# Row tiles of the seven-product stages: split three ahead into x's leftover tiles, loaded into four raw tiles

## The chip, the cores and the metric

One core of a Trainium2 chip. The metric is the device time of one execution in microseconds: 2548.99 us is the median of three runs before the change (2543.51 to 2549.86).

## The reference

One decoder layer of sliding-window attention, on x of 2048 tokens by 2048 channels, all float32:

```
h = rms_norm(x, swa_norm)
q, k, v, gate = split(h @ w_in, [2048, 2304, 2560])   # w_in 2048 x 4608, 32 query heads of 64, 4 key heads
q, k = rms_norm(q, q_gain), rms_norm(k, k_gain)       # per head
for each block of 128 queries, its keys being its own block and the one before:
    s = q @ k^T / 8 + bias[bucket(dist)], outside the window of 128: -inf
    m = max(max(s), sink); p = exp(s - m); p = p / (sum(p) + exp(sink - m))
    o = p @ v
x + (o * silu(gate)) @ w_out                          # w_out 2048 x 2048
```

The change touches two matrix products of it alone, each 2048 x 2048 x 2048: the gate's part of h @ w_in, and the last one with w_out.

## The kernel before

**Numbers in two parts.** Every float32 operand is split into a high part h (a copy rounded to TensorE's float32r format) and a low part l (the remainder, also float32r), and a product is the sum of three: h with h, h with l, l with h. For a row tile (128 output rows, held as the stationary operand) the parts are called wh and wl, made by `split_stat` (L123): for each half of 512 columns a copy on ScalarE (L133), then a subtraction on VectorE (L134). The moving operand's parts are called bigh and bigl, later obh and obl (`add_operand`, L536). `gemm` (L141) runs, for each k tile of 128, six matmuls of 128 x 512 columns: wh with the operand's high part (L148), wh with its low part (L151), wl with its high part (L154), each for two column halves.

**Two parts of the program.** In the first (up to about 1207 us) queries, keys and values are projected and attention runs beside the projections; its output goes to DRAM as `o_sp`. The second computes two large products one after the other: stage "g" (the gate projection, multiplied into `o_sp`, giving `o2_sp`) and stage "o" (times w_out, plus x). Each is done by a scheme with seven products of half size (1024 x 1024 x 1024) in place of eight, in the order b11, b21, t2, t3, t4, t1, b22 (L641). A product is named by its moving operand. Each has eight row tiles of 128 rows, and a row tile takes 8 k tiles x 6 = 48 matmuls into two accumulators of PSUM. In b11 and b21 of stage "g" the operand is what is left of x in SBUF from the projections; the other twelve operands are built by `prepare` (L564) while the product before them runs, one k tile beside each row tile.

**Row tiles.** `stationary` (L590) loads a row tile's raw values of 128 x 1024 (512 KB). For b11, b21 and t4 that is one load. For t3, t1 and b22 two loads are added or subtracted on VectorE (in the trace araw<-araw,a2raw, L498). For t2 three are loaded, one subtraction runs on GpSimd (L501), one addition on VectorE, and the sum is also stored to DRAM (`s2_sp`, L599), from where b22 fetches it again. The first raw tile comes from four buffers called raw, the second (a2raw) from four called rest: the buffers that hold the last two k tiles of x's second half until product b21 of stage "g" is done. Row tiles are loaded up to two products ahead (L667), in t2 of "g" only one ahead after the first. They are split when their own product is issued (L588), and wh and wl have three buffers of half a row tile each.

**Results.** Each product's accumulators are added to or stored as running sums (u in SBUF, u3 through DRAM). The products b21, t4, t1 and b22 also finish output tiles: in "g" by gating (VectorE, ScalarE, GpSimd, then a store of craw), in "o" by adding x (a load of x into craw, GpSimd, VectorE, then a store of craw; L639). PSUM has eight accumulators there, two for each row tile.

**The order.** Tiles come from pools with a fixed number of buffers. The program text gives the priority, a planner simulates the engines and puts every engine's instructions into one fixed order, and semaphores are added after that. All transfers are issued by SyncE (SP), in order: one that waits for a buffer holds those behind it. VectorE, ScalarE and GpSimd work in order as well.

The lines that the change touches besides `load_a2` (L510) and `product` (L586):

```
        if name == "t2":
            other = load_a if kind == "g" and i == 0 else load_a2
            a11, a21, a22 = [f(quarter_a(kind, mh, kh, i)) for f, mh, kh in ((other, 0, 0), (other, 1, 0), (load_a, 1, 1))]
...
        while made < min(len(tiles), m + 3) and not (made > m + 1 and tiles[made][0] == 2 and tiles[made][1] > 0):
            raws.append(stationary(*flat[tiles[made][0]], tiles[made][1]))
            made += 1
```

Of the kernel before, what the change touches and what calls it, by code (L numbers as in the profile page):

```python
# [16 lines left out]
P = 128  # L17
# [5 lines left out]
CH = 512  # L23
# [8 lines left out]
def swa_layer_kernel(ctx: ExitStack, tc: tile.TileContext, xT: bass.AP, x: bass.AP, w_in: bass.AP,  # L32
# [90 lines left out]
    def split_stat(raw, cuts=(0, HALF), eng=nc.vector):  # L123

        parts = []
        for n in range(2):
            h = st.tile([P, CH], F32R, tag="wh", name="wh", bufs=3)
            l = st.tile([P, CH], F32R, tag="wl", name="wl", bufs=3)
            for a, b in zip(cuts, cuts[1:]):
                a, b = max(a - n * CH, 0), min(b - n * CH, CH)  # L130
                if a < b:
                    r = raw[:, n * CH + a:n * CH + b]
                    nc.scalar.copy(out=h[:, a:b], in_=r)  # L133
                    eng.tensor_tensor(out=l[:, a:b], in0=r, in1=h[:, a:b].bitcast(F32), op=ALU.subtract)  # L134
            parts.append((h, l))
        return parts
# [4 lines left out]
    def gemm(stat, res, acc=None, ks=range(KT), last=KT - 1):  # L141
        if acc is None:
            acc = new_acc()
        for k in ks:
            h, l = stat[k // 4]
            cs = slice((k % 4) * P, (k % 4 + 1) * P)
            for n in range(2):
                nc.tensor.matmul(acc[n], h[:, cs], res[0][k][:, n * CH:(n + 1) * CH],  # L148
                                 start=(k == 0), stop=False)
            for n in range(2):  # L150
                nc.tensor.matmul(acc[n], h[:, cs], res[1][k][:, n * CH:(n + 1) * CH],  # L151
                                 start=False, stop=False)
            for n in range(2):
                nc.tensor.matmul(acc[n], l[:, cs], res[0][k][:, n * CH:(n + 1) * CH],  # L154
                                 start=False, stop=(k == last))
        return acc
# [346 lines left out]
    def bring(raw, src):  # L503
        nc.sync.dma_start(out=raw if len(src.shape) == 2 else raw.rearrange("p (k c) -> p k c", c=P), in_=src)  # L504
        return raw
# [1 line left out]
    def load_a(src):  # L507
        return bring(st.tile([P, HALF], F32, tag="raw", name="araw", bufs=RAW), src)

    def load_a2(src):  # L510
        return bring(rest.tile([P, HALF], F32, tag="rest", name="a2raw"), src)

    def load_b(src):
        return bring(gp.tile([P, HALF], F32, tag="braw", name="braw", bufs=3), src)

# [67 lines left out]
            vec(raw, raw, b, ALU.subtract)  # L583
        add_operand(ops, raw, scale if kind == "g" else None)

    def product(raw, ops, accs):  # L586
        acc = [accs.tile([P, CH], F32, tag="acc", name="acc") for _ in range(2)]
        return gemm(split_stat(raw), ops, acc, ks=range(8), last=7)  # L588

    def stationary(kind, name, i):  # L590

        if name in ("b11", "b21", "t4"):
            return load_a(quarter_a(kind, *{"b11": (0, 0), "b21": (0, 1), "t4": (1, 1)}[name], i))
        if name == "t2":
            other = load_a if kind == "g" and i == 0 else load_a2
            a11, a21, a22 = [f(quarter_a(kind, mh, kh, i)) for f, mh, kh in ((other, 0, 0), (other, 1, 0), (load_a, 1, 1))]
            pool(a11, a21, a11, ALU.subtract)
            vec(a22, a22, a11, ALU.add)
            nc.sync.dma_start(out=s2_sp[i], in_=a22)  # L599
            return a22  # L600
        a = load_a(quarter_a(kind, *{"t3": (0, 0), "t1": (1, 0), "b22": (0, 1)}[name], i))
        b = load_a2(s2_sp[i] if name == "b22" else quarter_a(kind, 1, int(name == "t1"), i))
        vec(a, a, b, ALU.add if name == "t1" else ALU.subtract)
        return a

# [42 lines left out]
    flat = [(kind, name) for kind in stages for name in ORDER]  # L648
    u = {}
    tiles = [(p, i) for p in range(len(flat)) for i in range(M8)]  # L650
    raws, made = [], 0
    for m, (p, i) in enumerate(tiles):
        kind, name = flat[p]
        stage = stages[kind]
        if i == 0:
            nxt = (res[0][8:], res[1][8:]) if p == 0 else ([], [])
            if kind == "g" and name in ("b21", "t1"):
                rbs[int(name == "t1")] = load_rb(int(name == "b21"))
        if p == 0 and i in (0, 2):
            beside(len(steps) + i // 2)  # L660
        if p == 0 and i == 4:

            attention.close()
            gp = ctx.enter_context(tc.tile_pool(name="gp", bufs=1, reuse_waits="tile"))
            ps_acc2 = ctx.enter_context(tc.tile_pool(name="ps_acc2", bufs=4, space=PSUM, reuse_waits="tile"))

        while made < min(len(tiles), m + 3) and not (made > m + 1 and tiles[made][0] == 2 and tiles[made][1] > 0):  # L667
            raws.append(stationary(*flat[tiles[made][0]], tiles[made][1]))
            made += 1
        raw = raws[m]  # L670
        if name == "b21" and i not in u:
            u[i] = gp.tile([P, HALF], F32, tag="u", name="u", bufs=M8)
            nc.sync.dma_start(out=u[i], in_=x1_sp[i])
        base = [u[i][:, n * CH:(n + 1) * CH] for n in range(2)] if i in u else None
        if name in ("t4", "t1"):
            u3 = [bring(evp.tile([P, CH], F32, tag="ev", name="u3"), u3_sp[i][:, n * CH:(n + 1) * CH]) for n in range(2)]
        if name in PUT:
            put = stage.begin(i, *PUT[name])
        if name == "b11":
            if i >= 4:  # L680
                sum_t2(kind, i - 4)
        if 0 < p < len(flat) - 1:
            prepare(*flat[p + 1], nxt, i)
        acc = product(raw, operand, ps_acc2 if gp is not None and i % 2 else ps_acc)
        if name == "b11" and gp is not None:
            u[i] = gp.tile([P, HALF], F32, tag="u", name="u", bufs=M8)
            base = [u[i][:, n * CH:(n + 1) * CH] for n in range(2)]
        for n in range(2):
            if name == "b11":
                if base:  # L690
                    nc.scalar.copy(out=base[n], in_=acc[n])
                else:
                    x1 = evp.tile([P, CH], F32, tag="ev", name="x1")
                    nc.scalar.copy(out=x1, in_=acc[n])
                    nc.sync.dma_start(out=x1_sp[i][:, n * CH:(n + 1) * CH], in_=x1)
            elif name == "t3":
                w = evp.tile([P, CH], F32, tag="ev", name="w")
                vec(w, acc[n], base[n], ALU.add)
                nc.sync.dma_start(out=u3_sp[i][:, n * CH:(n + 1) * CH], in_=w)
            else:  # L700
                if name in ("t2", "t1"):
                    vec(base[n], acc[n], base[n], ALU.add)
                if name in PUT:
                    stage.end((i, *PUT[name]), put[n], n, acc[n], u3[n] if name in ("t4", "t1") else base[n], name == "t4")
        if i == M8 - 1:
            operand = nxt
# [30 lines left out]
```

## Time and profile before

| | |
|---|---|
| median of 3 runs | 2548.99 us (2543.51 to 2549.86) |
| profiled execution | 2545.65 us, its span 2543.9 us |
| TensorE (PE) matmuls, busy | 2453.2 us, 96% of the span |
| VectorE (DVE) | 1655.1 us, 65% |
| GpSimd (POOL) | 1031.1 us, 41% |
| ScalarE (ACT) | 972.4 us, 38% |
| DMA through SP's queue | 427.14 MB, 51.7% of 16 engines' span |
| mean granted clock of TensorE | 0.988 |

Busy shares are means over the whole span. PE's matmuls overlap, so its busy time is not work at its peak. The second part, which the change touches, lasts from 1207 us to the end at 2543.9. A row of instructions shows the idle time of its engine just before it and, behind an arrow, what ended the idle time.

### The profile page before, as it was taken

The numbers are of one execution on the slowest core, as the hardware profiler recorded it, in microseconds if no ns is written. First come the engines' busy times: TensorE is split into PE (matmuls) and PEld (weight loads), VectorE is DVE, ScalarE is ACT, GpSimd is POOL, SyncE is SP. The second block draws the span as 40 slices with busy tenths as digits, with TensorE's granted clock in tenths as the row PEclk, the third lists the DMA queues.
The fourth block names the chain that finished last, engine by engine and source line by source line (L and its number), as shares of the span: only waits on it lengthen the run. The fifth ranks groups of instructions, "written<-read, shape, count | busy, mean of one in ns | idle before, by whom it ended". The sixth has DMA issues, their size and how long they took to land. (4 is left out here: it accounts for less than half of the span.)

```text
span 2543.9 us, 35165 instructions
## 1 busy us (share of the span) xinstructions
PE 2453.2 (96%) x11858; PEld 2043.9 (80%) x11858; DVE 1655.1 (65%) x3220; ACT 972.4 (38%) x2387; POOL 1031.1 (41%) x1011
## 2 busy tenths in 40 slices
PE   7999999999899999999999899999999989998899
PEld 5788888887788888888878688877788877787777
DVE  7387875789787786778747674676763445544532
ACT  6265664456555554455533321231332111121110
POOL 8366665666666666566522300122231120012222
PEclk9999999999999999999999899999999999999999
DMA  5433342125321214122248986887776786767753
GB/s 191 132 101 95 101 132 85 53 83 177 104 82 52 82 55 136 51 64 82 81 170 303 360 280 217 267 257 249 228 252 233 253 261 223 250 221 242 264 174 108
DMA packets 209076, 429.39 MB, mean 169 GB/s; under 512 B 19952, under 2 KB 91264, under 8 KB 208896
## 3 DMA queue, kind: packets, MB, share of 16 engines
q1 hardware_dynamic: 208896, 427.14, 51.7%
q8 instruction: 94, 1.54, 0.2%
q14 instruction: 86, 0.70, 0.1%
HBM read 336.88 MB, written 90.19 MB: 168 GB/s over the span
## 5 line engine op out<-in xcount | busy, mean ns | idle before, releaser
L154 PE MATMUL acc<-obh,wl 128*128 128x512 f32 x1536 | 481.6, 395 | 44.9 <-DVE wl L134 44.6
L148 PE MATMUL acc<-bigh,wh 128*128 128x512 f32 x1536 | 503.0, 397 | 14.6 <-ACT bigh L101 9.5
L151 PE MATMUL acc<-bigl,wh 128*128 128x512 f32 x1536 | 499.8, 397 | 3.6 <-DVE bigl L102 3.2
L154 PE MATMUL acc<-bigh,wl 128*128 128x512 f32 x1536 | 496.0, 395 | 1.0 <-DVE wl L134 1.0
L148 PE MATMUL acc<-obh,wh 128*128 128x512 f32 x1536 | 479.1, 393 | 10.3 <-ACT wh L133 10.2
L151 PE MATMUL acc<-obl,wh 128*128 128x512 f32 x1536 | 477.1, 392 | 0.0
L154 PEld LDWEIGHTS acc<-obh,wl 128*128 128x128 f32 x1536 | 288.5, 190 | 117.0 <-DVE wl L134 58.5
L148 PEld LDWEIGHTS acc<-obh,wh 128*128 128x128 f32 x1536 | 291.3, 190 | 73.4 <-ACT wh L133 11.9
L148 PEld LDWEIGHTS acc<-bigh,wh 128*128 128x128 f32 x1536 | 286.1, 190 | 71.1 <-ACT bigh L101 11.6
L151 PEld LDWEIGHTS acc<-obl,wh 128*128 128x128 f32 x1536 | 291.4, 190 | 61.8
L151 PEld LDWEIGHTS acc<-bigl,wh 128*128 128x128 f32 x1536 | 285.7, 190 | 59.5 <-DVE bigl L102 8.4
L154 PEld LDWEIGHTS acc<-bigh,wl 128*128 128x128 f32 x1536 | 286.3, 190 | 56.5 <-DVE wl L134 2.8
L133 ACT CAST wh<-araw 128x512 fp32r<-128x512 f32 x224 | 136.8, 619 | 484.2 <-PE acc L151 459.4
L501 POOL TENSOR_TENSOR craw<-craw,u 128x512 f32<-128x512 f32 x64 | 89.4, 1410 | 468.2 <-DMA craw<-x 277.5
L355 ACT ACTIVATE lg<-lg,nm 128x128 f32<-128x128 f32 x512 | 199.9, 392 | 194.3 <-DVE nm L348 190.6
L501 POOL TENSOR_TENSOR craw<-craw,th 128x512 f32<-128x512 f32 x64 | 96.8, 1531 | 437.3 <-DVE th L620 368.9
L134 POOL TENSOR_TENSOR wl<-raw,wh 128x512 fp32r<-128x512 f32 x148 | 193.8, 1310 | 108.3 <-ACT wh L133 96.7
L134 DVE TENSOR_TENSOR wl<-araw,wh 128x512 fp32r<-128x512 f32 x224 | 175.3, 789 | 77.0 <-ACT wh L133 75.3
L498 DVE TENSOR_TENSOR araw<-araw,a2raw 128x1024 f32<-128x1024 f32 x63 | 80.8, 1285 | 212.0 <-DMA araw<-o_sp 136.5
L360 POOL TENSOR_TENSOR lg<-lg,den 128x512 f32<-128x512 f32 x128 | 135.8, 1061 | 108.4 <-DVE den L359 67.6
L544 ACT CAST obh<-braw 128x1024 fp32r<-128x1024 f32 x80 | 84.2, 1052 | 244.0 <-DVE braw L498 119.2
L342 DVE SCALAR_TENSOR_TENSOR lg<-s,rq,bias 128x128 f32<-128x128 f32 x512 | 144.9, 343 | 39.5 <-PE pt L364 23.3
(117 smaller groups left out, 3496.2 us busy)
## 6 DMA issues: line engine op xcount, KB each, us to landing
braw<-w_out SPq DMA_DIRECT2D x88, 512.0 KB, 5.9
raw<-w_in SPq DMA_DIRECT2D x79, 512.0 KB, 3.7
braw<-xT SPq DMA_DIRECT2D x72, 512.0 KB, 5.3
araw<-w_in SPq DMA_DIRECT2D x58, 512.0 KB, 5.5
araw<-o_sp SPq DMA_DIRECT2D x56, 512.0 KB, 5.5
o_sp<-og SPq DMA_DIRECT2D x128, 128.0 KB, 1.9
craw<-o_sp SPq DMA_DIRECT2D x64, 256.0 KB, 4.2
o_sp<-craw SPq DMA_DIRECT2D x64, 256.0 KB, 4.7
```

The costliest lines, as they stand in the source:

```text
L133: nc.scalar.copy(out=h[:, a:b], in_=r)
L134: eng.tensor_tensor(out=l[:, a:b], in0=r, in1=h[:, a:b].bitcast(F32), op=ALU.subtract)
L148: nc.tensor.matmul(acc[n], h[:, cs], res[0][k][:, n * CH:(n + 1) * CH], start=(k == 0), stop=False)
L151: nc.tensor.matmul(acc[n], h[:, cs], res[1][k][:, n * CH:(n + 1) * CH], start=False, stop=False)
L154: nc.tensor.matmul(acc[n], l[:, cs], res[0][k][:, n * CH:(n + 1) * CH], start=False, stop=(k == last))
L342: nc.vector.scalar_tensor_tensor(out=lg[:, b, h], in0=s[:, b, h, P:], scalar=r, in1=bt[:, h, :], op0=ALU.mult, op1=ALU.add)
L355: nc.scalar.activation(out=lg[:, b, h], in_=lg[:, b, h], func=AF.Exp, bias=nm[:, b, h:h + 1], accum_out=den[:, b, h:h + 1])
L360: nc.gpsimd.tensor_tensor(out=lf, in0=lf, in1=den.rearrange("p b h -> p (b h)").unsqueeze(2).broadcast_to([P, 4, P]), op=ALU.mult)
L498: nc.vector.tensor_tensor(out=out, in0=a, in1=b, op=op)
L501: nc.gpsimd.tensor_tensor(out=out, in0=a, in1=b, op=op)
L544: nc.scalar.copy(out=h, in_=src)
```

## The change

Row tiles of products from t2 of "g" on are split by a new function `split_a`. It puts the first half's parts into wh and wl as before, and the second half's parts, high and low together, into one tile of rest. The raw tiles of a row tile all come from the four raw buffers; `load_a2` is gone. Row tiles are loaded up to three products ahead (index below m + 4) and split up to two ahead (below m + 3), for all products; in b11 and b21 of "g" the split is the old one, since rest still holds x there.

```diff
-    def load_a2(src):
-        return bring(rest.tile([P, HALF], F32, tag="rest", name="a2raw"), src)
...
-    def product(raw, ops, accs):
+    def split_a(raw):
+        parts = []
+        for n in range(2):
+            if n:
+                both = rest.tile([P, 2, CH], F32R, tag="rest", name="parts")
+                h, l = both[:, 0], both[:, 1]
+            else:
+                h = st.tile([P, CH], F32R, tag="wh", name="wh", bufs=3)
+                l = st.tile([P, CH], F32R, tag="wl", name="wl", bufs=3)
+            r = raw[:, n * CH:(n + 1) * CH]
+            nc.scalar.copy(out=h, in_=r)
+            vec(l, r, h.bitcast(F32), ALU.subtract)
+            parts.append((h, l))
+        return parts
+
+    def product(parts, ops, accs):
         acc = [accs.tile([P, CH], F32, tag="acc", name="acc") for _ in range(2)]
-        return gemm(split_stat(raw), ops, acc, ks=range(8), last=7)
+        return gemm(parts, ops, acc, ks=range(8), last=7)
...
-            other = load_a if kind == "g" and i == 0 else load_a2
-            a11, a21, a22 = [f(quarter_a(kind, mh, kh, i)) for f, mh, kh in ((other, 0, 0), (other, 1, 0), (load_a, 1, 1))]
+            a11, a21, a22 = [load_a(quarter_a(kind, mh, kh, i)) for mh, kh in ((0, 0), (1, 0), (1, 1))]
...
-        b = load_a2(s2_sp[i] if name == "b22" else quarter_a(kind, 1, int(name == "t1"), i))
+        b = load_a(s2_sp[i] if name == "b22" else quarter_a(kind, 1, int(name == "t1"), i))
...
-        while made < min(len(tiles), m + 3) and not (made > m + 1 and tiles[made][0] == 2 and tiles[made][1] > 0):
-            raws.append(stationary(*flat[tiles[made][0]], tiles[made][1]))
-            made += 1
-        raw = raws[m]
+        while len(raws) < min(len(tiles), m + 4):
+            raws.append(stationary(*flat[tiles[len(raws)][0]], tiles[len(raws)][1]))
+            if len(parts) < min(len(raws) - 1, m + 3):
+                parts.append((split_stat if tiles[len(parts)][0] < 2 else split_a)(raws[len(parts)]))
+        while len(parts) < min(len(tiles), m + 3):
+            parts.append((split_stat if tiles[len(parts)][0] < 2 else split_a)(raws[len(parts)]))
...
-        acc = product(raw, operand, ps_acc2 if gp is not None and i % 2 else ps_acc)
+        acc = product(parts[m], operand, ps_acc2 if gp is not None and i % 2 else ps_acc)
```

## Rows read from the trace of the kernel before

**Rows 1.** Page, costliest groups: busy, mean ns | idle before, releaser.
```profile
L154 PE MATMUL acc<-obh,wl 128*128 128x512 f32 x1536 | 481.6, 395 | 44.9 <-DVE wl L134 44.6
...
L148 PE MATMUL acc<-obh,wh 128*128 128x512 f32 x1536 | 479.1, 393 | 10.3 <-ACT wh L133 10.2
```
**Rows 2.** Windows: length, busy PE, PEld, DVE, ACT, POOL (instructions), PEclk, DMA share, GB/s.
```profile
1329.30:1416.30 87.00, 87.00 (x385) 72.06 (x384) 63.37 (x73) 30.49 (x43) 21.38 (x13) 1.00 0.92 316
1416.30:1518.50 102.20, 91.20 (x386) 74.34 (x384) 68.35 (x72) 31.01 (x39) 23.63 (x11) 0.93 0.91 320
...
1692.60:1790.30 97.70, 90.03 (x385) 72.82 (x384) 71.58 (x92) 27.14 (x41) 24.89 (x16) 0.98 0.81 260
1790.30:1883.50 93.20, 88.95 (x385) 71.61 (x384) 69.83 (x91) 29.55 (x45) 25.94 (x18) 1.00 0.73 219
...
1970.60:2066.20 95.60, 90.69 (x385) 73.86 (x384) 33.50 (x41) 15.90 (x23) 23.06 (x15) 0.96 0.76 243
2066.20:2164.00 97.80, 90.55 (x386) 72.79 (x385) 55.52 (x64) 17.46 (x24) 5.61 (x3) 0.98 0.75 249
2164.00:2254.20 90.20, 87.83 (x386) 71.83 (x385) 46.04 (x55) 18.95 (x26) 0.00 (x0) 1.00 0.65 216
2254.20:2344.60 90.40, 87.67 (x386) 71.93 (x385) 38.59 (x43) 17.64 (x24) 22.39 (x16) 1.00 0.79 263
2344.60:2450.90 106.30, 92.34 (x386) 73.80 (x385) 50.32 (x64) 17.13 (x24) 21.86 (x16) 0.97 0.70 230
2450.90:2543.90 93.00, 87.86 (x385) 71.75 (x383) 31.31 (x44) 8.46 (x14) 21.07 (x16) 0.99 0.37 129
```
**Rows 3.** Timeline at the end: start, us, engine, line, operation.
```profile
2539.21 0.61 PE L154 MATMUL acc<-obh,wl 128*128 128x512 f32 x2
```
**Rows 4.** Window of the first slow matmuls of g t2, columns as rows 2.
```profile
1437.20:1446.20 9.00, 7.85 (x18) 5.68 (x19) 6.88 (x7) 2.24 (x3) 2.12 (x2) 0.50 1.05 401
```
**Rows 5.** Waits, whole trace: us in total, times, longest us.
```profile
DVE araw L498 <- DMA araw<-o_sp: 136.5, 23, 12.3
...
PE acc L154 <- DVE wl L134: 45.6, 30, 4.7
```
**Rows 6.** Timeline of o t1, VectorE and SP's queue (SPq), columns as rows 3.
```profile
2397.11 1.23 DVE L498 TENSOR_TENSOR araw<-araw,a2raw 128x1024 f32<-128x1024 f32 x1 [8.49 <-DMA araw<-o_sp]
...
2411.52 1.23 DVE L498 TENSOR_TENSOR araw<-araw,a2raw 128x1024 f32<-128x1024 f32 x1 [9.59 <-issue]
...
2436.51 1.23 DVE L498 TENSOR_TENSOR araw<-araw,a2raw 128x1024 f32<-128x1024 f32 x1 [8.48 <-issue]
...
2438.97 1.53 SPq L639 DMA_DIRECT2D out<-craw  x2
...
2440.05 1.28 DVE L134 TENSOR_TENSOR wl<-araw,wh 128x512 fp32r<-128x512 f32 x2
2441.99 0.93 SPq L504 DMA_DIRECT2D craw<-x  x2
...
2443.02 0.38 SPq L504 DMA_DIRECT2D araw<-o_sp  x1
...
2448.14 1.23 DVE L498 TENSOR_TENSOR araw<-araw,a2raw 128x1024 f32<-128x1024 f32 x1 [6.80 <-DMA araw<-o_sp]
```
**Rows 7.** Timeline of SP's queue at the start of g t2.
```profile
1423.14 1.20 SPq L504 DMA_DIRECT2D a2raw<-w_in  x2
```
**Rows 8.** Timeline of PE behind the first row tile of g t2.
```profile
1437.20 1.22 PE L148 MATMUL acc<-obh,wh 128*128 128x512 f32 x2 [9.86 <-ACT wh L133]
```
**Rows 9.** DMA issues, whole trace: count, KB each, median us to landing.
```profile
araw<-o_sp SPq DMA_DIRECT2D x56, 512.0 KB, 5.5
...
a2raw<-w_in SPq DMA_DIRECT2D x30, 512.0 KB, 8.0
```
**Rows 10.** Groups by line, whole trace: busy us, mean ns | idle before.
```profile
L498 DVE TENSOR_TENSOR araw<-araw,a2raw 128x1024 f32<-128x1024 f32 x63 | 80.8, 1285 | 212.0 <-DMA araw<-o_sp 136.5 <-DMA araw<-w_in 45.1 <-issue 30.3
...
L501 POOL TENSOR_TENSOR a2raw<-a2raw 128x1024 f32<-128x1024 f32 x15 | 37.7, 2516 | 86.7 <-DMA a2raw<-o_sp 40.6 <-DMA a2raw<-w_in 30.4 <-DMA braw<-w_out 15.8
```

More of the change, by code (lines that the diff above doesn't have):

```diff
@@ L650, in swa_layer_kernel @@
     tiles = [(p, i) for p in range(len(flat)) for i in range(M8)]
-    raws, made = [], 0
+    raws, parts = [], []
     for m, (p, i) in enumerate(tiles):
```

## The prediction

> **What bounds the kernel now.** I went from the page's groups to windows, to waits, to the timeline. TensorE is busy 96% of the span, but it also waits: of its groups in the seven-product stages two have idle time worth naming, the third matmul pair of a k tile, which needs the low part wl (44.9 us), and the first, which needs the high part wh (10.3 us) [rows 1]. So PE waits for the split of a row tile, which is made just ahead of its use.
>
> The windows, one for each product of eight row tiles (384 matmuls; cut where the first matmul with the product's operand starts), say where. A product that waits for nothing takes 87.0 us, 10.88 us a row tile [rows 2], as b21 of "g" shows (g t3, g t4 and o b11 read 87.0 to 87.1 too). Over 87.0 are, in order: g t2 15.2, g t1 10.7, g b22 6.2, o b21 8.6, o t2 10.8, o t3 3.2, o t4 3.4, o t1 19.3, o b22 6.0 [rows 2]: 83.4 us. Of that 55.2 is idle time [rows 1]; 4.3 lies behind the last matmuls (their pair starts at 2539.21 and takes 0.45 like any other, the span ends at 2543.9) [rows 3]; the rest, some 24, is matmuls at the lower clock after an idle stretch: between 1437.2 and 1446.2 the granted clock was 0.50, and 18 matmuls ran where 40 run at full speed [rows 4]. So an idle microsecond costs about 1.4. At most 83.4 - 4.3 = 79 us can be had. The product g b11 (1207 to 1329) is left out, since the attention's last matmuls run in it.
>
> Why is wl late? VectorE works in order, and the add that makes a row tile (araw<-araw,a2raw) stands there waiting for its load: 136.5 us in 23 waits, the longest 12.3, while PE waits for wl 30 times [rows 5]. Of three wh and three wl buffers a row tile uses two each, so only half a row tile can stand ready, 5.4 us of cover.
>
> One turn of this, in o t1 [rows 6]: add at 2436.51; four evacuations up to 2440.05; two wl; the out stores from 2438.97; SP then stands until a store has landed to load craw (2441.99), and only behind that issues the araw load (2443.02); it lands 5.1 us later, and the next add starts at 2448.14. A turn takes 11.6 us here and 14.4 from 2397.11 to 2411.52, where PE needs 10.88. It goes round through SP and VectorE whatever stands ready for PE.
>
> At g t2 the cause is another: a2raw tiles are those that x's last k tiles leave, so the loads of the second row tile go out at 1423 and later, behind the end of b21 (1416.3) [rows 7], and PE stands 9.86 us [rows 8]. With the clock of rows 4 (9.0 us for 18 matmuls, 4.9 too many) that is nearly all of the 15.2; the other row tiles of g t2 ran at 10.88.
>
> **The change, part by part.**
>
> *Parts ready.* From t2 on the second half's parts go to the rest tiles, so 3 wh, 3 wl and 3 of the 4 rest tiles hold three row tiles: while one is multiplied two stand ready, 21.8 us of cover instead of about 5.4. No instruction is added or removed: the same two copies, two subtractions, loads and add. ScalarE's and VectorE's sums stay (VectorE is 71.6 us busy in the 97.7 of g t1, its fullest product [rows 2]).
>
> *What is moved.* Each row tile is brought one product earlier, and with it one to three loads of 512 KB, the add, and in t2 the subtraction on GpSimd (2.5 us, ahead of a gate's multiplication) and a 512 KB store in SP's queue. Per stage the bytes are the same, but in b21 of "g", at 316 GB/s and a DMA share of 0.92 [rows 2], one more row tile is 2 MB, 6 us of transfers in front of the operand's. That costs 0 to 6; I count it in g t2 below.
>
> *A wait is added.* The second half of the first t2 row tiles needs a rest tile, free only when b21's last k tile has been multiplied at 1416.3. Behind that copy on ScalarE stands the operand's next copy. PE needs this half 24 matmuls (5.4 us) into the product, and the work is a copy and a subtraction under 1.3 us each: 0 to 2 us. I take 0; the first half hides it.
>
> *Raw tiles.* All loads of row tiles now share four raw tiles, against four raw and four rest, and a t2 row tile takes three. Its turn, from the nearest rows: load 5.5 to 8.0 us [rows 9], subtraction 2.5, add 1.3 [rows 10]: 9.3 to 11.8 us, against 10.88. A load that waits for a raw tile stands on SP in front of operand loads, base loads and stores.
>
> The Trainium skill (DMA: Bandwidth & Descriptors, section Anatomy of one DMA) fits 2.0 us plus the bytes over 436 GB/s to a transfer of the GpSimd path, an estimate of 3.2 us for 512 KB. By it the turn would be 7.0 us, four raw tiles would be plenty, and g t2 would keep nothing below. The transfers of rows 9 went through SP and took 5.5 to 8.0; the measurement decides.
>
> *What is left of each stall:*
> - g t2, 15.2 now: the loads no longer wait for rest tiles, so the second row tile should be there at 1427. But cover hasn't built up, and seven turns 0.9 us too long make 6.3. Between 0 and 15 I take 6.
> - g t1 and b22, 16.9 now: VectorE's turn loses 0.7 to 3.5 us a product, over 16 adds 11 to 56. Against it stand 21.8 us of ready parts, and on the other side PSUM: eight accumulators, two a row tile, so evacuations may fall some three products (33 us) behind before PE feels it. Left 0 to 17; the DMA share is 0.73 to 0.81, against 0.91 in g t2, so nearer the short turn: 5.
> - o b21 to o t4, 26.0 now: a few turns with craw, then t2's three-load turns, with the cover full at the start. Left 0 to 26; I take 9.
> - o t1 and b22, 25.3 now, of them 4.3 behind the last matmul: the same turn for 16 adds. Beside the 4.3 I take 10, since VectorE's lateness also shows at the end, where few products are left to catch up in.
>
> Late next would be the operand's last two k tiles, whose buffers come free with the last row tile's first matmuls: two copies and two subtractions in the 17.7 us from there to PE's need. I take nothing for it.
>
> Left 6 + 5 + 9 + 14.3 = 34.3 of 83.4; gone 49. The profiled execution took 2545.65 us (span 2543.9), so it becomes 2496.6. The median shown, 2548.99, is 3.3 above it; for the median I predict 2500.
>
> **The rivals.**
>
> A, *everything is covered.* All 79 us go: 2470. For it: the idle time hangs on wh and wl alone [rows 1], and 21.8 us of cover exceed the longest single wait, 12.3 [rows 5]. Against: the waits follow each other turn after turn.
>
> B, *the turn is the bound, and cover is spent once.* Where adds and evacuations alternate, PE ends at the turn's pace. Gone are g t2's 15.2 less 6 and half a cover's worth elsewhere, some 20 us: 2529. For it: the chain of rows 6 doesn't pass through the wh buffers. Against: such stretches last 8 to 16 products, about what cover and PSUM hold.
>
> C, *no change, or stalls merely move* to the operand's last k tiles, or into g b11, where splits now go ahead of the attention's last units: 2541 to 2557. For it: the three instructions of the turn stay in one queue. Against: 30 waits of PE are for wl itself.
>
> D, *slower: four raw tiles bind.* In t2, t3, t1 and b22 a row tile's last load can go out only when an earlier row tile has been split, so load, add, evacuation and split follow each other: 8.0 + 1.3 + 2.3 + 1.3 is 12.9, and with SP held by waiting stores 14. In four runs of 16 row tiles (t2 with t3, t1 with b22, in either stage) with d us too much each, PE loses 4 x (16 d - 21.8). That exceeds 79 from d = 2.6, a turn of 13.5 us; at 14 (d = 3.1) it is 111 lost against 79 gained: 2581. For it: a2raw from w_in takes 8.0 us, and half the buffers are gone. Against: the loads of "o" take 5.5.
>
> **How the numbers follow.** Forecast 2500 (by itself 2482 to 2518) 0.43; A 0.18; B 0.15; C 0.09; D 0.15. The range of 80% runs from a little below A, 2466, to the middle of C, 2547; D and the upper half of C are outside. A measurement of this kernel tells about 0.3% (8 us) from no change. Faster by more: the forecast, A and B, 0.76. Within it: C, 0.09. Slower: D, 0.15.
>
> **What the changed profile would show.** Windows near 87 us for g t1, g b22 and o b21 to o t4; no idle time of PE's third pair on wl; no hole of 10 us behind the first t2 row tile; the clock at 1.00 in more windows; wh copies that wait for PE more than a product ahead of use. B shows as adds on VectorE 12 to 14 us apart, with PE waiting for wl or for evacuations late in o t1 and b22. D shows as SP waiting for wl in front of araw loads, and t2 windows over 100 us. Waits of PE for obh or obl would mean that the operand is late next. The prediction is wrong if the time stays above 2541, or if stages other than g t2 keep what they lose now.

## The result, and the profile after

The changed kernel takes 2508.36 us (median of 4 runs, 2503.99 to 2515.92), the kernel before, beside it on the same chip, 2546.25 (4 runs, 2538.34 to 2549.86). The ratio is 0.9858, with a 95% interval of 0.9822 to 0.9895: about 38 us faster, 8 short of the 2500 predicted. The profiled execution took 2505.3 us, its span 2503.6 (before 2543.9).

The page after, busy time of each engine with its share of the span:
```profile
PE 2437.5 (97%) x11858; PEld 2042.5 (82%) x11858; DVE 1657.0 (66%) x3220; ACT 970.6 (39%) x2387; POOL 1038.5 (41%) x1011
...
L151 PE MATMUL acc<-obl,parts 128*128 128x512 f32 x768 | 240.1, 394 | 26.7 <-DVE obl L498 17.7
...
L154 PE MATMUL acc<-obh,wl 128*128 128x512 f32 x768 | 236.6, 389 | 0.1
...
L148 PE MATMUL acc<-obh,wh 128*128 128x512 f32 x768 | 236.4, 389 | 0.0
```
The engines do the same work as before. What is gone is idle time in front of the matmuls: the pair that needs wl stood 44.9 us before and the pair that needs wh 10.3 [rows 1]; now 0.1 and 0.0, and beside them the second halves' pairs (named parts) wait little for their own split. A new wait has come: the pair L151, for the operand's low part obl.

The waits of PE after, those that belong to the second part of the program (us in total, times, longest):
```profile
PE acc L151 <- DVE obl L498: 17.7, 2, 14.3
...
PE acc L151 <- DVE obl L539: 8.9, 1, 8.9
...
PE acc L154 <- DVE parts L498: 1.9, 1, 1.9
PE acc L148 <- ACT parts L594: 1.5, 1, 1.5
```
Of the thirty waits for wl [rows 5], 28 with 44.6 us lay in the second part; none is left there (the trace still has 1.3 us of them, all before 1207). In their place are five waits for obl and parts, 30.0 us in all, each in a product's first row tile. The windows by product, cut as before (columns as in [rows 2]): g t2, g t1, g b22, o b21, o t2, o t3, o t4, o t1, o b22, and behind them two short ones, from the end of the longest wait on:
```profile
1415.80:1508.80 93.00, 89.46 (x385) 72.95 (x384) 68.75 (x76) 32.32 (x42) 22.32 (x10) 0.98 0.94 328
...
1682.90:1769.90 87.00, 87.00 (x385) 72.08 (x384) 63.95 (x82) 21.90 (x34) 22.40 (x14) 1.00 0.83 264
1769.90:1868.00 98.10, 89.15 (x385) 73.36 (x384) 77.95 (x103) 34.11 (x51) 31.66 (x20) 0.95 0.80 246
...
1955.00:2042.10 87.10, 87.10 (x386) 72.12 (x386) 34.37 (x41) 15.68 (x23) 21.36 (x13) 1.00 0.79 261
2042.10:2134.40 92.30, 88.94 (x385) 73.13 (x384) 51.87 (x57) 16.93 (x24) 14.89 (x7) 0.98 0.81 273
2134.40:2221.60 87.20, 87.20 (x385) 72.00 (x384) 50.93 (x61) 18.53 (x25) 0.00 (x0) 1.00 0.72 238
2221.60:2308.70 87.10, 87.10 (x386) 72.11 (x385) 42.46 (x44) 17.87 (x24) 22.76 (x16) 1.00 0.84 282
2308.70:2395.70 87.00, 87.00 (x385) 72.04 (x384) 42.57 (x53) 16.39 (x23) 16.70 (x12) 1.00 0.74 243
2395.70:2503.60 107.90, 89.43 (x385) 73.25 (x383) 35.32 (x49) 6.13 (x10) 25.88 (x20) 0.93 0.44 146
...
2418.80:2427.80 9.00, 8.99 (x31) 7.28 (x32) 3.53 (x5) 0.62 (x1) 2.58 (x2) 0.77 0.43 135
2427.80:2434.00 6.20, 6.20 (x29) 5.14 (x28) 2.98 (x5) 0.62 (x1) 0.00 (x0) 1.00 0.67 202
```
Five of the nine stages that lost time run at 87 now. Over 87.0 are g t2 6.0, g b22 11.1, o t2 5.3, o b22 20.9 (4.3 of it still behind the last matmuls) and 0.4 in o b21, o t3 and o t4 together: 43.7 us where 83.4 were, so 39.7 less; the span fell by 40.3. o b22 got worse by 14.9, g b22 by 4.9.

What happened at the start of o b22 stands in the timelines of VectorE, ScalarE, SP's queue and PE (start, us, engine, line, operation):
```profile
2387.79 1.23 DVE L498 TENSOR_TENSOR araw<-araw 128x1024 f32<-128x1024 f32 x1 [8.41 <-DMA araw<-s_sp]
...
2400.75 1.23 DVE L498 TENSOR_TENSOR araw<-araw 128x1024 f32<-128x1024 f32 x1 [8.14 <-DMA araw<-s_sp]
2401.89 0.68 DVE L498 TENSOR_TENSOR u<-acc,u 128x512 f32<-128x512 f32 x1
...
2413.41 1.22 DVE L498 TENSOR_TENSOR araw<-araw 128x1024 f32<-128x1024 f32 x1 [7.84 <-DMA araw<-s_sp]
...
2417.54 2.35 DVE L498 TENSOR_TENSOR obl<-braw,obh 128x1024 fp32r<-128x1024 f32 x2
```
```profile
2389.62 2.00 ACT L541 CAST obh<-braw 128x1024 fp32r<-128x1024 f32 x2
```
```profile
2403.20 1.54 SPq L651 DMA_DIRECT2D out<-craw  x2
2407.39 0.98 SPq L504 DMA_DIRECT2D craw<-x  x2
2408.47 0.38 SPq L504 DMA_DIRECT2D araw<-s_sp  x1
```
```profile
2418.81 1.22 PE L151 MATMUL acc<-obl,parts 128*128 128x512 f32 x2 [14.34 <-DVE obl L498]
```
The last two high parts of the operand were ready on ScalarE at 2391.6. Their low parts came 26 us later, at 2417.54, though one takes 1.2: in VectorE's fixed order they stand behind two more row-tile adds and the evacuations between them. Those adds are 13.0 and 12.7 apart, because the turn that [rows 6] showed is still there: stores of craw at 2403.20, SP stands until one has landed (2407.39), the load of the stored sum goes out behind that (2408.47), and the add starts when it is there (2413.41). PE multiplied ready row tiles meanwhile and lost nothing, until it came to k tiles whose low part had not been made.

### The profile page after: what moved, and what is told of

It is laid out like the page before. It is cut to its first block, busy times and chain, and to the rows that moved or that the text cites. A ratio compares the mean times of both kernels' runs of the same rounds, so it can differ in the third digit from the quotient of the medians.

```text
span 2503.6 us, 35188 instructions
## 1 busy us (share of the span) xinstructions
PE 2437.5 (97%) x11858; PEld 2042.5 (82%) x11858; DVE 1657.0 (66%) x3220; ACT 970.6 (39%) x2387; POOL 1038.5 (41%) x1011
## 5 line engine op out<-in xcount | busy, mean ns | idle before, releaser
L151 PE MATMUL acc<-bigl,wh 128*128 128x512 f32 x1536 | 499.2, 397 | 3.1 <-DVE bigl L102 3.0
L151 PEld LDWEIGHTS acc<-bigl,wh 128*128 128x128 f32 x1536 | 285.5, 190 | 58.5 <-DVE bigl L102 7.1
L501 POOL TENSOR_TENSOR craw<-craw,th 128x512 f32<-128x512 f32 x64 | 103.1, 1631 | 410.8 <-DVE th L632 332.7
L151 PE MATMUL acc<-obl,parts 128*128 128x512 f32 x768 | 240.1, 394 | 26.7 <-DVE obl L498 17.7
L154 PE MATMUL acc<-obh,parts 128*128 128x512 f32 x768 | 239.0, 393 | 1.9 <-DVE parts L498 1.9
L148 PE MATMUL acc<-obh,parts 128*128 128x512 f32 x768 | 238.3, 392 | 1.5 <-ACT parts L594 1.5
L154 PE MATMUL acc<-obh,wl 128*128 128x512 f32 x768 | 236.6, 389 | 0.1
L151 PE MATMUL acc<-obl,wh 128*128 128x512 f32 x768 | 236.5, 389 | 0.0
L148 PE MATMUL acc<-obh,wh 128*128 128x512 f32 x768 | 236.4, 389 | 0.0
L498 DVE TENSOR_TENSOR araw<-araw 128x1024 f32<-128x1024 f32 x64 | 80.0, 1249 | 205.6 <-DMA araw<-s_sp 83.4
L151 PEld LDWEIGHTS acc<-obl,parts 128*128 128x128 f32 x768 | 145.5, 190 | 58.4 <-DVE obl L498 18.8
L154 PEld LDWEIGHTS acc<-obh,parts 128*128 128x128 f32 x768 | 146.1, 190 | 33.0 <-DVE parts L498 2.4
L148 PEld LDWEIGHTS acc<-obh,parts 128*128 128x128 f32 x768 | 145.3, 189 | 32.2 <-ACT parts L594 1.9
```

Of the source, the lines that this page charges most:

```text
L498: nc.vector.tensor_tensor(out=out, in0=a, in1=b, op=op)
L501: nc.gpsimd.tensor_tensor(out=out, in0=a, in1=b, op=op)
```

## The experiments

Each ratio is to the kernel before, run on the same chip. The theory was this: the cover works, the turn of VectorE and SP stands, and its lateness comes out at the operand's last low parts; what holds the turn is SP's order. Rivals: the depth of the cover is too small; the operand's buffers come free too late; raw tiles are too few; g t2 alone is what was gained.

**The parts of the change by themselves.** First the kernel before, with one edit that keeps its buffers but loads the second t2 row tile of "g" into raw tiles, one product earlier:
```diff
-            other = load_a if kind == "g" and i == 0 else load_a2
+            other = load_a if kind == "g" and i < 2 else load_a2
...
-        while made < min(len(tiles), m + 3) and not (made > m + 1 and tiles[made][0] == 2 and tiles[made][1] > 0):
+        while made < min(len(tiles), m + 3) and not (made > m + 1 and tiles[made][0] == 2 and tiles[made][1] > 1):
```


> The kernel before, with one edit: the second row tile of g t2 also takes its three loads from the raw buffers and may be loaded ahead, as the first does; nothing stands ready split. Theory (two separate gains: a hole at g t2 from buffers that were not free, and the cover): g t2 falls from 102.2 to 88 to 93, the products with waits for wl stay as before (g t1 98, o t1 106, o t2 98), so 2531 to 2538 against 2546. Rival (one gain: only parts that stand ready help): g t2 stays at 100 or more, 2546.

2538.35 against 2547.68 us, 0.9952 (0.9935 to 0.9969). Its window for g t2:
```profile
1414.90:1505.30 90.40, 88.22 (x386) 71.76 (x385) 62.75 (x69) 28.18 (x37) 21.70 (x10) 1.00 0.93 343
```
The hole in g t2 (PE's stand of 9.86 us [rows 8]) is a gain of its own, 102.2 to 90.4, and needs none of the cover. The other stages keep their stalls (g t1 takes 100.1, o t1 104.1). It is a quarter to a third of what the whole change gives (9 of 38 us by the medians, 0.5 of 1.4% by the ratios).

Then the raw tiles alone: all loads in the four raw tiles, no cover.
```diff
-        return bring(rest.tile([P, HALF], F32, tag="rest", name="a2raw"), src)
+        return load_a(src)
...
-        while made < min(len(tiles), m + 3) and not (made > m + 1 and tiles[made][0] == 2 and tiles[made][1] > 0):
+        while made < min(len(tiles), m + 4):
```


> The kernel before, with all row-tile loads in the four raw buffers and up to three products ahead, but row tiles split as before, when their own product is issued: the change's raw tiles without its parts. Theory (four raw tiles cost little, cover does the work): waits for wl stay as before or are somewhat longer, g t2 loses the hole; 2530 to 2555. Rival (four raw tiles bind, D of the prediction): without cover the turns of 12 to 14 us show in t2, t3, t1 and b22 of both stages; slower than before by 30 us or more, 2575 to 2650.

2547.27 against 2547.68, 0.9995 (0.9982 to 1.0008). Windows of g t3 and o t2:
```profile
1505.10:1600.80 95.70, 90.22 (x386) 72.84 (x385) 52.83 (x62) 19.06 (x26) 0.00 (x0) 0.98 0.67 222
...
2050.00:2155.80 105.80, 92.97 (x386) 74.12 (x385) 54.09 (x63) 17.52 (x24) 16.40 (x7) 0.95 0.75 254
```
g t2 falls to 90.0, and g t3 (87.0 before) and o t2 (97.8) take it back; PE's waits for wl in the second part stay at 44.6 us, in 35 waits. So four raw tiles (and loads one row tile further ahead) do cost something, some 9 to 12 us without cover, far from what rival D needs; the rest of the gain is the cover's.

The depth, with the changed kernel one row tile shallower in loads and in splits (where "ahead" is counted in products, one row tile's product is meant; the change splits two row tiles ahead of the one in work, and the title's three counts that one too):
```diff
-        while len(raws) < min(len(tiles), m + 4):
+        while len(raws) < min(len(tiles), m + 3):
...
-            if len(parts) < min(len(raws) - 1, m + 3):
+            if len(parts) < min(len(raws) - 1, m + 2):
...
-        while len(parts) < min(len(tiles), m + 3):
+        while len(parts) < min(len(tiles), m + 2):
```


> The changed kernel with one product less ahead in the program: row tiles loaded up to two products ahead and split up to one ahead, same buffers. Since the program's order only gives priority and buffers bound what is done ahead, theory: nearly no difference, 2500 to 2512, products without waits stay at 87. Rival (the depth named in the change does the work): waits for wl come back in g t1, o t2 and o t1, 2520 to 2540.

2512.62 against 2549.19, 0.9848 (0.9831 to 0.9865), not told apart from the change. g b22 takes 98.5, o b22 109.4, t1 still 87. So the depth in the program's text isn't what gives the cover. The buffers for parts are what is left to give it; a kernel that splits ahead without them was not run.

**The new wait.** Is it the turn, or buffers of the operand that come free late? In the next kernel b22's stored sum is neither loaded nor added (the kernel leaves this part of the computation out, with 16 loads of 512 KB), so that the turn has no add in b22:
```diff
         a = load_a(quarter_a(kind, *{"t3": (0, 0), "t1": (1, 0), "b22": (0, 1)}[name], i))
+        if name == "b22":
+            return a
```


> The changed kernel, but the row tiles of b22, in both stages, are their first load alone: the stored sum isn't fetched and not added, so part of the computation is left out (16 loads of 512 KB and 16 adds on VectorE). No matmul, no operand and no buffer is changed. Theory (the turn): the adds that VectorE waits with during t1 and b22 are gone, so it isn't behind when the operand's last two low parts come: the stalls at g b22 (11.1) and o b22 (16.6) go, windows 87 and 91.3; 2478 to 2484 us. Rival (buffers): the last two k tiles are as late as before, g b22 98 and o b22 108 stay, 2505.

2481.7 against 2549.19, 0.9736 (0.9719 to 0.9752). Windows of g b22 and o b22:
```profile
1767.10:1854.10 87.00, 87.00 (x386) 72.04 (x385) 64.60 (x85) 29.19 (x44) 26.57 (x18) 1.00 0.74 229
...
2386.70:2478.10 91.40, 87.24 (x385) 71.92 (x384) 23.97 (x33) 6.24 (x10) 23.83 (x18) 1.00 0.38 127
```
Both stalls in front of obl are gone, and only the 4.3 behind the last matmuls is left. The operand's buffers are as before, so it is the adds, with the loads that they wait for, that obl stands behind. o t2, whose adds stayed, kept its stall, and it grew (95.2 against 92.3).

If so, another engine might make these low parts past VectorE's order. The last two k tiles' subtraction goes to GpSimd:
```diff
+        low = pool if len(ops[0]) >= 6 else vec
...
-            vec(l, src, h.bitcast(F32), ALU.subtract)
+            low(l, src, h.bitcast(F32), ALU.subtract)
```


> The changed kernel, but the low part of an operand's last two k tiles is subtracted on GpSimd where it needs no gain (g t2 to t4, all of stage o); in g t1 and g b22, where a gain is multiplied in, it stays on VectorE. Theory (the turn, VectorE behind): the stalls at o t2 (5.3) and o b22 (16.6) go or shrink to a few us, since GpSimd isn't behind; g b22 keeps its 11; 2487 to 2495 us, unless GpSimd's own wait for craw holds the subtraction. Rival (buffers): GpSimd gets the high part just as late and takes longer for the subtraction, so the stalls stay or grow: 2508 to 2515.

2509.91 against 2547.68, 0.9843 (0.9828 to 0.9857): no gain over the change. The expectation missed, but for the exception that it named, GpSimd's own wait for craw. GpSimd around the end of the wait:
```profile
2403.75 2.54 POOL L501 TENSOR_TENSOR craw<-craw,u 128x512 f32<-128x512 f32 x2 [9.80 <-DMA craw<-x]
...
2416.36 2.48 POOL L501 TENSOR_TENSOR craw<-craw,u 128x512 f32<-128x512 f32 x2 [10.06 <-DMA craw<-x]
...
2418.79 5.66 POOL L501 TENSOR_TENSOR obl<-braw,obh 128x1024 fp32r<-128x1024 f32 x2
```
In this kernel obh was copied at 2395.64. From there to obl's start on GpSimd are 23 us (in the change, from the copy's start at 2389.62, 28 on VectorE), behind two pairs of craw additions 12.6 apart, and PE waited 15.5 us (14.3): GpSimd takes part in the same turn, through the loads of craw. Leaving VectorE is not enough; the turn must get shorter.

**What holds the turn.** Transfers of the evacuations leave SP in three steps. The loads of x into craw (stage "o") are issued by GpSimd (`bring` and `load_c` pass the engine on, here and below):
```diff
-    def load_c(src):
+    def load_c(src, eng=nc.sync):
...
-            return [load_c(self.part(x, at, n)) for n in range(2)]
+            return [load_c(self.part(x, at, n), nc.gpsimd) for n in range(2)]
```


> The changed kernel, but in stage o the loads of x into craw are issued by GpSimd, which also uses them, and not by SP; VectorE's order moves in a few places, ScalarE's and TensorE's not at all. Theory (the turn): what is left over 87 us a product (o t2 5.3, o b22 16.6 beside the 4.3 behind the last matmul, g b22 11.1) is VectorE running behind, since add, evacuation, store, craw load, row-tile load and the next add go round in 12.9 us; it comes out at the operand's last two low parts, which stand behind those adds. With craw off SP the o turn should fall to about 10 us: o t2 about 87, o b22 about 91.3, g b22 98 as now, 2487 us. Rival (buffers): the last two k tiles are late because their buffers come free late; then all windows stay, 2508. Rival (four raw tiles): a load waits for a split whatever SP does; adds stay 12 us or more apart and o b22 stays above 100, 2500 to 2508.

2503.47 against 2547.68, 0.9818 (0.9797 to 0.984). Windows of o t2 and o b22:
```profile
2045.60:2132.70 87.10, 87.10 (x386) 72.10 (x385) 52.53 (x57) 16.95 (x24) 15.26 (x10) 1.00 0.83 283
...
2393.80:2500.90 107.10, 89.40 (x385) 73.23 (x383) 37.99 (x50) 6.12 (x10) 37.90 (x40) 0.93 0.48 160
```
Half a hit. o t2's stall is gone. Around the start of o b22 the adds are still up to 12.4 apart, and the wait stays (13.5 us), as the rival of the raw tiles had it; that rival is tried below.

Then the running sum's loads (u) as well, in stage "o":
```diff
-            u3 = [bring(evp.tile([P, CH], F32, tag="ev", name="u3"), u3_sp[i][:, n * CH:(n + 1) * CH]) for n in range(2)]
+            u3 = [bring(evp.tile([P, CH], F32, tag="ev", name="u3"), u3_sp[i][:, n * CH:(n + 1) * CH], nc.gpsimd if kind == "o" else nc.sync) for n in range(2)]
```


> The changed kernel, but in stage o the loads that evacuations need, x into craw and the stored sums into u, are issued by GpSimd; stores and row tiles stay with SP, g stays as it is. Theory (SP's waits for craw and for u hold the turn together): SP has only the out stores in front of a row tile's load, a turn of about 10.5; o t2 87, o b22 91 to 96, g b22 98 as now: 2483 to 2492. Rival (stores alone are enough to hold it): o b22 above 100, 2500 to 2508.

2493.69 against 2550.41, 0.9767 (0.975 to 0.9783). The adds of o t1 come 11.0 to 12.0 apart, and o b22 takes 99.7, less than before and more than the 91 to 96 expected:
```profile
2392.30:2492.00 99.70, 89.91 (x385) 73.58 (x383) 37.48 (x49) 6.23 (x10) 37.32 (x38) 0.96 0.45 148
```
And the same in both stages:
```diff
-            return [load_c(o_sp[mh * 8 + i][:, (1 - nh) * HALF + n * CH:(1 - nh) * HALF + (n + 1) * CH]) for n in range(2)]
+            return [load_c(o_sp[mh * 8 + i][:, (1 - nh) * HALF + n * CH:(1 - nh) * HALF + (n + 1) * CH], nc.gpsimd) for n in range(2)]
...
-            u3 = [bring(evp.tile([P, CH], F32, tag="ev", name="u3"), u3_sp[i][:, n * CH:(n + 1) * CH]) for n in range(2)]
+            u3 = [bring(evp.tile([P, CH], F32, tag="ev", name="u3"), u3_sp[i][:, n * CH:(n + 1) * CH], nc.gpsimd) for n in range(2)]
```

> As the kernel with the evacuations' loads on GpSimd, but in both stages: in g the loads of the attention's output into craw and of u too. Theory: g b22 falls from 98 to 87 to 92 as well, 2475 to 2485 us. Rival (in g the gates' own chain over VectorE, ScalarE and GpSimd sets the turn, and GpSimd now also waits for loads): g t1 or g b22 get longer, 2495 or more.

2492.32 against 2550.41, 0.9769 (0.9755 to 0.9784), the same: a miss. g b22 takes 100.4 and PE waits 8.9 for obl there, as in the change. In "g" the craw and u loads alone do not hold the turn. SP's queue and VectorE in g t1 of this kernel show what does once they are gone:
```profile
1759.36 0.33 SPq L504 DMA_DIRECT2D araw<-w_in  x1
1766.31 0.34 SPq L504 DMA_DIRECT2D araw<-s_sp  x1
```
```profile
1764.87 1.41 DVE L498 TENSOR_TENSOR wl<-araw,wh 128x512 fp32r<-128x512 f32 x1
...
1770.11 1.23 DVE L498 TENSOR_TENSOR araw<-araw 128x1024 f32<-128x1024 f32 x1 [3.83 <-DMA araw<-s_sp]
```
SP issues nothing between 1759.7 and 1766.3 and sends the load of the stored sum the moment the split that reads an older raw tile ends (1764.87 + 1.41). So in "g" a load does wait for a raw tile, as rival D had it, and the split that frees it stands behind the gating on VectorE (which is 78.0 us busy in the change's g b22, its fullest product).

The rival that raw tiles hold it in "o" too: the second load of t3, t1 and b22 takes a rest tile again, with craw and u back on SP.
```diff
+    def load_a2(src):
+        return bring(rest.tile([P, HALF], F32, tag="rest", name="a2raw"), src)
...
-        b = load_a(s2_sp[i] if name == "b22" else quarter_a(kind, 1, int(name == "t1"), i))
+        b = load_a2(s2_sp[i] if name == "b22" else quarter_a(kind, 1, int(name == "t1"), i))
```


> The changed kernel, but the second load of a row tile of t3, t1 and b22 goes into the fourth rest tile, which three row tiles' parts leave free, and not into the four raw ones. Theory (two things hold the turn: SP behind craw, and a load that waits for a split's raw tile): the split no longer stands in the chain of a second load, but SP's waits for craw do; the turn falls by about 1 us, g b22 (no x there) loses most of its 11, o b22 stays above 100; 2492 to 2502. Rival (the raw tiles alone are the cause): o b22 falls to 91 too, 2480. Rival (raw tiles don't matter): 2508, all windows as now.

2510.1 against 2549.19, 0.9841 (0.982 to 0.9862), no gain, less than the 2492 to 2502 expected. VectorE's adds at the end of o t1:
```profile
2376.71 1.22 DVE L498 TENSOR_TENSOR araw<-araw,a2raw 128x1024 f32<-128x1024 f32 x1 [7.30 <-DMA a2raw<-o_sp]
2389.67 1.23 DVE L498 TENSOR_TENSOR araw<-araw,a2raw 128x1024 f32<-128x1024 f32 x1 [7.32 <-DMA a2raw<-s_sp]
```
13.0 apart, as before. The second load goes out at 2383.54, right behind the load of u at 2381.87 (1.57 us to issue): it waits for its turn on SP and not for a tile. And in the change itself SP does not wait once for a split in o t1 or o b22 (in the other products 66.8 us, in 45 waits). So in "o" the raw tile isn't what the load waits for. In "g" this kernel gains nothing either (g b22 99.4), but there the loads of craw were still with SP; no run took both away in "g". Then this together with craw by GpSimd, and in "o" a rest tile for one load of t2 too:
```diff
-            a11, a21, a22 = [load_a(quarter_a(kind, mh, kh, i)) for mh, kh in ((0, 0), (1, 0), (1, 1))]
+            a11, a21, a22 = [f(quarter_a(kind, mh, kh, i)) for f, mh, kh in
+                             ((load_a, 0, 0), (load_a if kind == "g" else load_a2, 1, 0), (load_a, 1, 1))]
...
-            return [load_c(self.part(x, at, n)) for n in range(2)]
+            return [load_c(self.part(x, at, n), nc.gpsimd) for n in range(2)]
```

> The changed kernel with both: craw's loads of x issued by GpSimd in stage o, and the second loads of t3, t1, b22 (in o also of t2) into the rest buffers. Theory (both hold the turn): o t2 87, o b22 91 to 95, g b22 87 to 92; 2475 to 2488 us. Rival (something else, as VectorE's own work or the evacuations, sets the 12 us): o b22 stays above 100, 2495 to 2505.

2514.61 against 2549.19, 0.9863 (0.9846 to 0.9881): missed, and slower than craw by GpSimd alone. SP's queue in o t1 shows what stands in the way:
```profile
2381.64 1.57 SPq L504 DMA_DIRECT2D u<-u_sp  x2
2383.30 0.50 SPq L504 DMA_DIRECT2D a2raw<-s_sp  x1
```
The load of the row tile now stands behind the load of u, whose buffer comes free with GpSimd's addition (2380.33 to about 2382.9). One blocker left SP and the next took its place. Why this kernel loses 11 us against craw by GpSimd alone, with other products longer (o t1 93.6, g b22 101.3), is not explained by this.

So the row tiles' own loads were taken out of SP's order: ScalarE issues them, nothing else changes.
```diff
     def load_a(src):
-        return bring(st.tile([P, HALF], F32, tag="raw", name="araw", bufs=RAW), src)
+        return bring(st.tile([P, HALF], F32, tag="raw", name="araw", bufs=RAW), src, nc.scalar)
```


> The changed kernel, but all loads of row tiles are issued by ScalarE and not by SP, so they don't stand behind stores and loads that wait for evacuations (out, craw, u). Theory (the turn goes round through SP's order): what is left of the turn is add 1.2, evacuation 2.4, split 1.3, issue 0.5, landing 4.7, about 10.1 us, under the 10.88 of PE; adds 10.9 apart, o t2, g b22 and o b22 lose their waits for obl, 2475 to 2485 us. Rival (VectorE's own chain or the landing times set the 12 to 13 us): adds stay 12 us or more apart, 2500 to 2510. Rival (ScalarE takes SP's place: its copies of obh and of parts now stand behind loads that wait for a raw tile): waits for obh or parts appear, 2500 or more.

2485.83 against 2550.41, 0.975 (0.9726 to 0.9774): at the edge of the 2475 to 2485 expected and faster than the change, whose interval it does not touch. Windows of g b22, o t2 and o b22, then VectorE's adds in o t1:
```profile
1771.50:1864.50 93.00, 89.27 (x386) 72.86 (x385) 72.75 (x96) 34.05 (x51) 30.79 (x20) 0.98 0.81 248
...
2038.60:2125.60 87.00, 87.00 (x385) 72.04 (x384) 49.68 (x54) 16.21 (x23) 11.71 (x5) 1.00 0.81 278
...
2386.70:2479.60 92.90, 87.52 (x385) 71.81 (x383) 32.15 (x42) 8.96 (x14) 27.51 (x20) 0.99 0.46 154
```
```profile
2348.83 1.23 DVE L498 TENSOR_TENSOR araw<-araw 128x1024 f32<-128x1024 f32 x1 [6.51 <-DMA araw<-s_sp]
2359.94 1.23 DVE L498 TENSOR_TENSOR araw<-araw 128x1024 f32<-128x1024 f32 x1 [5.08 <-DMA araw<-s_sp]
2369.57 1.23 DVE L498 TENSOR_TENSOR araw<-araw 128x1024 f32<-128x1024 f32 x1 [4.76 <-DMA araw<-s_sp]
```
The adds that come before the operand's last low parts are 8.8 to 12.7 apart, the three shown 9.6 to 11.1, about PE's 10.88. o b22 loses only 5.9, 4.3 of it the tail; g t3 loses 1.9 and g t2 still 5.1. In "o" it was SP's order that held the turn. In g b22 PE still waits 1.8 us for obh and 2.0 for obl; the first is the sign of the rival that ScalarE takes SP's place, the second goes with adds still 12 us apart at the end of g t1, where the load again goes out the moment a split ends (1774.36 and 1774.39).

Last, g t2's first row tile, with row_act: it is split the old way, into wh and wl, which needs no rest tile.
```diff
-                parts.append((split_stat if tiles[len(parts)][0] < 2 else split_a)(raws[len(parts)]))
+                parts.append((split_stat if len(parts) <= 2 * M8 else split_a)(raws[len(parts)]))
```


> The kernel with row-tile loads on ScalarE, and the first row tile of g t2 split with the old split, both halves into wh and wl, so that it needs no rest tile. Theory (the changed kernel's 6.0 us at g t2, 5.1 there now, are the second half's wait for a rest tile that x leaves only at the product's start, with two engines' queues behind it): g t2 falls from 92 to 87 or 88, nothing else moves, some 5 us less than without the edit, 2478 to 2483. Rival (g t2's transfers or VectorE are simply late there): g t2 stays at 91 or more, or the second row tile waits in its place; 2484 to 2488.

2483.68 against 2550.48, 0.9743 (0.972 to 0.9765), not told apart from the run before. Windows of g b21 and g t2:
```profile
1328.40:1417.30 88.90, 87.35 (x386) 72.02 (x385) 66.37 (x73) 30.15 (x42) 26.77 (x14) 1.00 0.91 312
1417.30:1506.60 89.30, 87.61 (x385) 71.92 (x384) 68.51 (x69) 29.69 (x40) 22.03 (x10) 1.00 0.93 316
```
g t2 falls from 92.1 to 89.3, but b21 rises from 87.0 to 88.9: its last row tile now shares the three wh and wl buffers, and PE waits 1.5 us for its wh. The wait on the rest tile was real, and a part of it only moves. "Nothing else moves" did not hold: in the profiles o b22 takes 97.7 here against 92.9, with waits for obh and obl of 1.1 and 2.1 us where one of 1.3 was; why, no run shows.

## Why the prediction was right or wrong

**Right: what bounded the kernel, and what the change removes.** PE waited for the split made just ahead of use. With parts ready, the waits for wl in the second part fell from 44.6 us to none, and t1, t3, t4 and b21 run at 87. The kernel with four raw tiles and no cover keeps these waits (44.6), so the cover is the cause. The g t2 hole is separate, as the prediction had it; alone it gave 9 of the 38 us.

**Right: the turn stays.** The prediction said that it goes round through SP and VectorE whatever stands ready for PE. After, the adds that make b22's row tiles are 12.7 to 13.2 apart from the end of o t1 into o b22 (the three before them 10.0 to 11.0). Rival A had the cover right and rival B the turn. The place where the two meet, the operand's last k tiles, stood in rival C, which let the whole gain move there: 33 us moved, of some 79.

**Wrong: "Late next would be the operand's last two k tiles ... I take nothing for it."** This term was named, and sized at 0; it measured 33.0 us (g b22 11.1, o t2 5.3, o b22 16.6), 26.6 of it PE's waits for obl. The working counted two copies and two subtractions against 17.7 us, as if VectorE came to them at once. But they stand in its order where the program put them, between adds that each wait for a load. Before, PE waited at every turn and was late with VectorE, and it never waited for obl in these stages; with two row tiles of cover PE runs on, and the whole lateness is paid at the first thing that the cover doesn't hold.

**The other terms.** What was to be left of the turn showed at that place only:

| left over 87.0 | predicted | measured |
|---|---|---|
| g t2 | 6 | 6.0 |
| g t1 and b22 | 5 | 11.1 |
| o b21 to o t4 | 9 | 5.7 |
| o t1 and b22, with the tail | 14.3 | 20.9 |
| sum | 34.3 | 43.7 |

Without g t2 and the tail, 24.0 were to be left as waits for wl spread over eight products; 33.0 are left, nearly all as waits for obl at the start of three. So a term that was too small and terms that were too large partly cancel, and the total is 9 off: that 2500 came so near 2508 is in part luck.

PSUM's accumulators, which were to let evacuations fall 33 us behind, did so, nearly to the end. The addition at 2401.89 above belongs to the sixth row tile of o t1, which PE had finished at about 2374.0. So from 2395.7, when b22 began, to about 2404 four row tiles held all eight accumulators, and the eighth row tile, finished at 2395.7, was not added until 2427.10, 31 us later. PE never waited for an accumulator, but little was left.

**g t2: the right sum for the wrong reason.** The 6 us were to come from seven turns of t2's three loads. The seven other row tiles ran at 10.88. The loss is the added wait that was "0 to 2; I take 0":
```profile
1423.34 0.73 PE L148 MATMUL acc<-obh,parts 128*128 128x512 f32 x2 [1.46 <-ACT parts L594]
...
1426.48 1.22 PE L154 MATMUL acc<-obh,parts 128*128 128x512 f32 x2 [1.95 <-DVE parts L498]
```
PE stands 1.46 and 1.95 us in the first row tile. The copy into the rest tile started at 1422.69 on ScalarE, behind two th activations and a multiplication by the gain, its subtraction at 1425.75 on VectorE, behind a gain multiplication of 2.30. The work was short, as the bound said; the queue ahead of it was not counted. That 6 met 6.0 is luck.

**Rival D (four raw tiles bind).** Its price was wrong: without cover they cost some 9 to 12 us over the whole second part, and with cover t2, t3 and t1 of both stages, after g t2, run within 5.3 us of 87. Its sign was there, SP waiting for a split in front of row-tile loads, and in "g", by the trace above, it holds the turn once the loads of craw and u have left SP. So it has a share in g b22's 11.1 that no run measured; a fifth raw tile was not tried.

**Open.** What keeps the rest of g b22 (93.0 with ScalarE's loads): the raw tile that a split frees late, behind the gating in VectorE's order, is the candidate, read from the traces and not tried by itself. ScalarE's late obh is another part of it.

## What to carry to other kernels

Cover for one consumer does not shorten the producer's loop: it moves the lateness to the next thing that the same in-order engine makes without cover. So when a term is "late next", look up where its instruction stands in its engine's order and count what waits ahead of it, not how long it takes. And when a loop runs over a queue of transfers, find the transfer that waits in front of the one that matters; here, moving the loads that matter out of that queue was worth more than half of what the change itself gave.

## What the runs showed of the hardware

Moving the row-tile loads from SP's queue to ScalarE's changed their count not at all and their landing little. Issues by the page, first after the change, then with ScalarE's loads (count, KB each, median us to landing):
```profile
araw<-o_sp SPq DMA_DIRECT2D x88, 512.0 KB, 5.5
```
```profile
araw<-o_sp ACTq DMA_DIRECT2D x88, 512.0 KB, 5.7
```
So what that kernel gained over the change (0.975 against 0.9858 of before, 22 us between the medians) is not in faster transfers, but in when they are issued.

In the changed kernel a long stall cost little more than a short one beyond itself. The loss beyond the idle time, in matmuls at a lower granted clock behind it, was 2.6 us in g t2 (3.4 idle, in two waits), 2.2 in g b22 (8.9), 1.9 in o t2 (3.4) and 2.3 in o b22 (14.3). The last is seen in the two short windows above: granted clock 0.77 in the first 9.0 us after the wait, when 31 matmuls ran that take 7.0 at 0.227 each, and 1.00 behind it. So the prediction's "about 1.4" per idle microsecond was not a rate: the two long waits cost 1.16 and 1.25 per idle microsecond, the two short ones 1.6 and 1.8. The loss is no fixed amount either: g t2 before lost 4.2 beyond its 11.0 idle (9.86 and, 3 us later, 1.14), with a granted clock of 0.50 over 9.0 us [rows 4].

GpSimd took 5.66 us for the two subtractions of 128x1024 with a float32r result (`obl`) for which VectorE took 2.35.
